# Stick-breaking attention with two heads per instruction, in PSUM tiles of two banks

## The chip, the cores and the metric

One core of a Trainium2 chip runs the whole program. Its engines are named as the profile names them: PE (TensorE, matmuls), PEld (the loading of its weights), DVE (VectorE), ACT (ScalarE), POOL (GpSimd) and SP (the engine whose queue issues most DMAs). Each engine works through its own queue in order. The metric is the time of one execution in microseconds (us).

## What is computed

Two transformer blocks over 512 tokens of width 1024, in f32: a mixer with two branches, a mixture of 16 experts, then a second block with retention, differential attention, cross attention and a feed-forward. The change touches one branch of the first mixer, stick-breaking attention with 8 heads of width 64 and blocks of 128 queries:

```python
def one_block(args):
    q_blk, blk = args
    z = jnp.einsum('bhqd,bhkd->bhqk', q_blk, k, preferred_element_type=jnp.float32) * scale
    q_pos = blk * QBLOCK + jnp.arange(QBLOCK)
    mask = key_pos[None, :] < q_pos[:, None]
    log_beta = jax.nn.log_sigmoid(z)
    log_keep = jnp.where(mask, jax.nn.log_sigmoid(-z), 0.0)
    later = jnp.concatenate([log_keep[..., 1:], jnp.zeros_like(log_keep[..., :1])], axis=-1)
    log_survive = lax.cumsum(later, axis=3, reverse=True)
    a = jnp.where(mask, jnp.exp(log_beta + log_survive), 0.0)
    return jnp.einsum('bhqk,bhkd->bhqd', a.astype(v.dtype), v)
```

The kernel uses that log_beta + log_survive = z minus the sum of softplus(z) over this key and all later ones.

## The kernel before

Products with weights are done in three float32r matmuls (high by high, high by low, low by high): `split` (lines 175 to 188) makes the two parts of a loaded weight, with a cast `whi` on ACT (L182) and a subtraction `wlo` on DVE (L183), each 128x1024; `mm3` (L200 to L202) issues the three matmuls; `hilo` (L265 to L267) splits an activation in the same way. `ws` (line 204) walks over tiles of 128 output columns, 24 matmuls of 512 columns each for the input projection. Below, a "filler" is one such matmul.

`sb_head` (lines 619 to 654) takes one head. Scores stand as keys by queries: for key block j (0 to 3) only the n = 512 - 128 j queries from that block on are computed, so a head has 512 + 384 + 256 + 128 = 1280 score columns. Per block: a score matmul (L628) in f32 over all 128 rows, where `sq_` holds one head's queries in 64 rows and zeros in the other 64; a bf16 matmul that adds the causal mask to the diagonal block (L629); a copy to `z` (L630, DVE); softplus as Abs, Exp, Ln on ACT (L632 to L634) and max-and-add on DVE (L635); the split into `ph` and `pl`. Then, per block, the running sum over later keys as matmuls with a triangle `tri` and ones `onesr` (L646, L647), the subtraction from z (L649, DVE), the exponential (L650, ACT), and the product with the values (L651, f32, 64 output rows).

`sb_head` runs for eight heads. Behind it in the program stand the gate projections (two `ws` of 8 tiles each, 384 fillers, evacuated by the ACT copies `gt`, L666), and then the two branch products (`w_branch_sb`, `w_branch_hg`). The instructions are not issued in program order: a scheduler of the framework puts each engine's queue in an order of its own, and so fillers of the gate projections stand between the matmuls of the heads. PSUM has 8 banks of 512 f32 columns: two each for the tags "mm" and "tp", and four that `four_banks` gives out again at each stage. The heads use those four singly (tag "at"). The second block's `diff_head` (line 1193) and `ret_pair` (line 1272) already take two heads at a time: score matmuls over 64 rows each (L1200, L1282), products with 64 output rows each (L1286), and one DVE instruction over both heads' banks (L1284).

Of the kernel before, what the change touches and what calls it, by code (L numbers as in the profile page):

```python
# [8 lines left out]
F32 = mybir.dt.float32  # L9
# [11 lines left out]
S = 512  # L21
# [7 lines left out]
NSL = 21  # L29
GX = (5, 6, 7, 8, 9)  # L30
# [53 lines left out]
def body(tc, a, out):  # L84
# [37 lines left out]
    def psum2():  # L122
        return banks[1][0].tile([128, 2, 512], F32, name="ps2", tag="at2", bufs=banks[1][2])
# [292 lines left out]
    slp = pool("slp", 1, stack=at)  # L416

    def slot(name):
        return slp.tile([128, S], F32, name=name, tag="sl", bufs=NSL)

# [165 lines left out]
    def ev_sq(t0):  # L586
        def f(t, o):
            for h in range(2):
                q = slot("sq")
                sq_[2 * (t0 + t) + h] = q  # L590
                G.memset(q[64 - 64 * h:128 - 64 * h, :], 0.0)
                A.activation(q[64 * h:64 * h + 64, :], o[64 * h:64 * h + 64, :], AF.Copy, scale=0.125)
        return f
# [18 lines left out]
    slp2 = pool("slp2", 1, stack=at)  # L612
    sbst = ExitStack()
    sb = pool("sb", 1, side="right", stack=sbst)
    COL = [0, 512, 896, 1152, 1280]

    last_exp = []

    def sb_head(h):
        t = h // 2  # L620
        z = sb.tile([128, 1280], F32, name="z", bufs=2)
        ph = sb.tile([128, 1280], F32R, name="ph", bufs=2)
        pl = sb.tile([128, 1280], F32R, name="pl", bufs=2)
        for j in range(4):
            n = S - 128 * j
            cc = slice(COL[j], COL[j + 1])
            o = psum("at")[:, :n]
            T.matmul(o, sk_[t][:, j * 128:(j + 1) * 128], sq_[h][:, j * 128:], start=True, stop=False)  # L628
            T.matmul(o[:, :128], identb, negsb, start=False, stop=True)  # L629
            V.tensor_copy(z[:, cc], o)  # L630
            e = sb.tile([128, S], F32, name="ea", bufs=3)[:, :n]
            A.activation(e, o, AF.Abs)  # L632
            A.activation(e, e, AF.Exp, scale=-1.0)
            A.activation(e, e, AF.Ln, bias=onec)  # L634
            V.scalar_tensor_tensor(e, z[:, cc], 0.0, e, op0=OP.max, op1=OP.add)  # L635
            hilo(ph[:, cc], pl[:, cc], e)
        y = psum("tp", name="ysbp")
        for j in range(4):
            n = S - 128 * j
            cc = slice(COL[j], COL[j + 1])  # L640
            o = psum("at")[:, :n]
            for i in range(j, 4):
                m = tri if i == j else onesr
                ci = slice(COL[i], COL[i + 1])
                oo = o[:, (i - j) * 128:]
                T.matmul(oo, m, ph[:, ci], start=(i == j), stop=False)  # L646
                T.matmul(oo, m, pl[:, ci], start=False, stop=(i == 3))  # L647
            w = sb.tile([128, S], F32, name="ea", bufs=3)[:, :n]
            V.tensor_sub(w, z[:, cc], o)  # L649
            last_exp[:] = [A.activation(w, w, AF.Exp)]  # L650
            T.matmul(y[64 * (h % 2):64 * (h % 2) + 64, 128 * j:], sv_[j][:, h * 64:(h + 1) * 64], w,  # L651
                     start=(j == 0), stop=(j == 3))
        p0 = 64 * (h % 2)
        hilo(ysb[0][p0:p0 + 64, t, :], ysb[1][p0:p0 + 64, t, :], y[p0:p0 + 64, :])

    for h in range(8):
        sb_head(h)
# [4 lines left out]
    def ev_gate(key):  # L662
        def f(t, o):
            n = t + (8 if key == "h" else 0)
            gt[key, t] = slot("gt") if n not in GX else slp2.tile([128, S], F32, name="gt2", bufs=len(GX))
            order(A.copy(gt[key, t], o), last_sk[0])  # L666
        return f
# [794 lines left out]
```

## Time and profile before

| | |
|---|---|
| runs | 1622.94, 1623.21, 1624.32 us, median 1623.21 |
| profiled execution | 1623.13 us |
| its span | 1621.3 us |
| busy in the span | PE 97%, PEld 75%, DVE 59%, ACT 51% |
| stick-breaking heads, 231.8 to 359.2 us | 127.4 us: PE 124.3, ACT 85.5, DVE 73.7 busy |
| the gate projections that are left, 359.2 to 391.4 us | 32.2 us: PE 32.2 busy |

A row of the profile gives an instruction's line, its engine, the tile written and the tiles read, and the shape. An f32 matmul shows as two records of one instruction, so its counts are double. A PE record lasts longer than its turn on the engine, since matmuls are pipelined: the turn is the distance from one start to the next. A bracket at the end of a timeline row gives the idle time of the engine before it and what ended it.

### The profile page before, as it was taken

How to read it: one execution, taken by the hardware profiler on the slowest of the kernel's cores; microseconds unless marked ns; L12 is line 12 of the kernel's file. 1: busy time of each engine (PE TensorE's matmuls, PEld its weight loads, DVE VectorE, ACT ScalarE, POOL GpSimd, SP SyncE). 2: the span in 40 equal slices, each digit the busy share in tenths (PEclk: the TensorE clock that was granted, in tenths of full speed). 3: DMA queues.
4: the chain of work that ended last, by engine and by line, in shares of the span. 5: the costliest groups of instructions: out<-in, count | busy, mean ns of one | idle time of the engine just before them, and what ended most of it. 6: DMA issues, size and time to landing. Idle time of an engine off the chain costs nothing. (4 is left out here: it accounts for less than half of the span.)

```text
span 1621.3 us, 20374 instructions
## 1 busy us (share of the span) xinstructions
PE 1579.7 (97%) x7631; PEld 1223.8 (75%) x7631; DVE 955.9 (59%) x1485; ACT 831.6 (51%) x1331; POOL 75.2 (5%) x92
## 2 busy tenths in 40 slices
PE   7999999999999999999989999999999999999999
PEld 6887776668878777776667667657878888888887
DVE  6459945643647899998855766456555433333221
ACT  5445556665335888888865664434444322323120
POOL 3000000000001211111110000000000000000000
PEclk9999999999999999999999999999999999999999
DMA  7230121123469999999974204224211333332331
GB/s 227 72 104 27 53 79 39 48 67 119 143 231 317 310 369 368 357 365 368 380 263 135 75 15 130 75 58 142 90 53 54 115 91 105 91 103 92 97 124 39
DMA packets 203070, 242.88 MB, mean 150 GB/s; under 512 B 10400, under 2 KB 133560, under 8 KB 202968
## 3 DMA queue, kind: packets, MB, share of 16 engines
q1 hardware_dynamic: 188800, 205.43, 38.1%
q0 software_dynamic: 7056, 24.27, 5.3%
q10 hardware_dynamic: 7112, 11.85, 2.5%
q8 instruction: 61, 1.00, 0.2%
q14 instruction: 41, 0.34, 0.1%
HBM read 223.69 MB, written 15.73 MB: 148 GB/s over the span
## 5 line engine op out<-in xcount | busy, mean ns | idle before, releaser
L183 DVE TENSOR_TENSOR wlo<-wraw,whi 128x1024 fp32r<-128x1024 f32 x210 | 256.0, 1223 | 284.9 <-ACT whi L182 275.5
L182 ACT CAST whi<-wraw 128x1024 fp32r<-128x1024 f32 x210 | 220.5, 1051 | 392.9 <-PE ps L201 276.2
L200 PE MATMUL ps<-hTh,whi 128*128 128x512 f32 (+1 forms) x912 | 349.8, 384 | 1.3 <-DVE fsg L1412 0.8
L201 PE MATMUL ps<-hTl,whi 128*128 128x512 f32 (+1 forms) x912 | 348.4, 382 | 0.8 <-DVE hTl L267 0.8
L202 PE MATMUL ps<-hTh,wlo 128*128 128x512 f32 (+1 forms) x912 | 347.7, 382 | 0.0
L183 DVE TENSOR_TENSOR wlo<-rx,whi 128x1024 fp32r<-128x1024 f32 x176 | 210.4, 1221 | 36.6 <-ACT whi L182 34.2
L182 ACT CAST whi<-rx 128x1024 fp32r<-128x1024 f32 x176 | 182.7, 1049 | 52.5 <-PE ps L202 31.3
L200 PEld LDWEIGHTS ps<-hTh,whi 128*128 128x128 f32 x912 | 172.2, 189 | 36.6 <-issue 3.3
L201 PEld LDWEIGHTS ps<-hTl,whi 128*128 128x128 f32 x912 | 172.2, 189 | 33.4 <-issue 2.2
L202 PEld LDWEIGHTS ps<-hTh,wlo 128*128 128x128 f32 x912 | 172.1, 189 | 31.3 <-issue 0.3
L200 PE MATMUL ps<-whi,XT 128*96 128x512 f32 x256 | 101.5, 396 | 1.8 <-ACTq L1045 1.8
L202 PE MATMUL ps<-whi,XT 128*96 128x512 f32 x256 | 102.0, 398 | 0.0
L201 PE MATMUL ps<-wlo,XT 128*96 128x512 f32 x256 | 100.9, 394 | 0.0
L200 PE MATMUL ps<-whi,hTh 128*128 128x512 f32 x192 | 77.4, 403 | 0.3 <-ACT hTh L266 0.2
L202 PE MATMUL ps<-whi,hTl 128*128 128x512 f32 x192 | 77.4, 403 | 0.0
L201 PE MATMUL ps<-wlo,hTh 128*128 128x512 f32 x192 | 76.6, 399 | 0.0
L200 PE MATMUL ps<-whi,aTh 128*128 128x512 f32 x176 | 68.5, 389 | 0.0
L202 PE MATMUL ps<-whi,aTl 128*128 128x512 f32 x176 | 68.5, 389 | 0.0
L201 PE MATMUL ps<-wlo,aTh 128*128 128x512 f32 x176 | 68.5, 389 | 0.0
L1412 DVE TENSOR_TENSOR fsg<-fsg,ps 128x512 f32<-128x512 f32 x22 | 15.1, 688 | 76.4 <-PE ps L202 76.4
L200 PEld LDWEIGHTS ps<-whi,XT 128*96 128x96 f32 x256 | 41.4, 162 | 18.4 <-ACTq L1045 2.2
L201 PEld LDWEIGHTS ps<-wlo,XT 128*96 128x96 f32 x256 | 41.5, 162 | 17.4 <-DVE wlo L183 0.3
(449 smaller groups left out, 2590.6 us busy)
## 6 DMA issues: line engine op xcount, KB each, us to landing
wraw<-in_w_in_dram SPq DMA_DIRECT2D x72, 512.0 KB
rx<-in_w_exp_gate_dram SPq DMA_DIRECT2D x58, 512.0 KB
rx<-in_w_exp_down_dram SPq DMA_DIRECT2D x58, 512.0 KB
rx<-in_w_exp_up_dram SPq DMA_DIRECT2D x52, 512.0 KB
wraw<-in_w_gate_dram SPq DMA_DIRECT2D x22, 512.0 KB
wraw<-in_w_up_dram SPq DMA_DIRECT2D x22, 512.0 KB
wraw<-in_w_down_dram SPq DMA_DIRECT2D x22, 512.0 KB
wraw<-in_w_out_dram SPq DMA_DIRECT2D x16, 512.0 KB
```

The source lines that it names most:

```text
L182: i1 = A.copy(hi, w)
L183: i2 = V.tensor_sub(lo, w, hi.bitcast(F32))
L200: T.matmul(o, lh, rh, start=first, stop=False)
L201: T.matmul(o, lh, rl, start=False, stop=False)
L202: T.matmul(o, ll, rh, start=False, stop=last)
L1412: V.tensor_mul(sg[t], sg[t], o)
```

## The change

Two heads now share an instruction. `sq_` keeps both heads of a pair as they come from the projection (one ACT instruction in place of two, no POOL memset), and the score matmuls of a pair read 64 rows each. Both write one PSUM tile of two banks (tag "sc"), and the running sums another (tag "run"); each tag has one buffer. The mask is added on DVE, in the instruction that moves the scores to `z`; Abs reads `z` in place of PSUM. Softplus, split, subtraction and exponential work on [128, 2, n], up to 1024 columns. The key blocks run from 3 to 0, each with its running sum and exponential, and the products with the values come after all four. `z`, `ph` and `pl` have two buffers for blocks 2 and 3 and one for blocks 0 and 1. The exponential is written over `z`. The gates take their slots from one pool.

```diff
-    def psum2():
-        return banks[1][0].tile([128, 2, 512], F32, name="ps2", tag="at2", bufs=banks[1][2])
+    def psum2(tag="at2"):
+        return banks[1][0].tile([128, 2, 512], F32, name=tag, tag=tag, bufs=banks[1][2])
...
+    mask = yp.tile([128, S], F32, name="mask")
+    G.memset(mask[:, 128:], 0.0)
+    V.tensor_copy(mask[:, :128], negsb)
...
-            for h in range(2):
-                q = slot("sq")
-                sq_[2 * (t0 + t) + h] = q
-                G.memset(q[64 - 64 * h:128 - 64 * h, :], 0.0)
-                A.activation(q[64 * h:64 * h + 64, :], o[64 * h:64 * h + 64, :], AF.Copy, scale=0.125)
+            sq_[t0 + t] = slot("sq")
+            A.activation(sq_[t0 + t], o, AF.Copy, scale=0.125)
...
+    four_banks("at1", 1)
...
+    def sb_pair(t):
+        y = psum("tp", name="ysbp")
+        z, ph, pl = {}, {}, {}
+        for j in (3, 2, 1, 0):
+            c0, n = 128 * j, S - 128 * j
+            o = psum2("sc")[:, :, :n]
+            for h in range(2):
+                T.matmul(o[:, h], sk_[t][hs[h], c0:c0 + 128], sq_[t][hs[h], c0:], start=True, stop=True)
+            z[j] = sb.tile([128, 2, n], F32, name=f"z{j}", bufs=2 if j > 1 else 1)
+            V.tensor_add(z[j], o, mask[:, None, :n].to_broadcast([128, 2, n]))
+            ph[j], pl[j] = (sb.tile([128, 2, n], F32R, name=f"p{q}{j}", bufs=2 if j > 1 else 1) for q in "hl")
+            e = sb.tile([128, 2, S], F32, name="ea", bufs=2)[:, :, :n]
+            A.activation(e, z[j], AF.Abs)
+            A.activation(e, e, AF.Exp, scale=-1.0)
+            A.activation(e, e, AF.Ln, bias=onec)
+            V.scalar_tensor_tensor(e, z[j], 0.0, e, op0=OP.max, op1=OP.add)
+            hilo(ph[j], pl[j], e)
+            o = psum2("run")[:, :, :n]
+            for h in range(2):
+                for i in range(j, 4):
+                    m = tri if i == j else onesr
+                    oo = o[:, h, (i - j) * 128:]
+                    T.matmul(oo, m, ph[i][:, h], start=(i == j), stop=False)
+                    T.matmul(oo, m, pl[i][:, h], start=False, stop=(i == 3))
+            V.tensor_sub(z[j], z[j], o)
+            last_exp[:] = [A.activation(z[j], z[j], AF.Exp)]
+        for j in range(4):
+            for h in range(2):
+                T.matmul(y[hs[h], 128 * j:], sv_[j][:, (2 * t + h) * 64:(2 * t + h + 1) * 64], z[j][:, h],
+                         start=(j == 0), stop=(j == 3))
+        hilo(ysb[0][:, t, :], ysb[1][:, t, :], y)
...
+    four_banks("at2")
```

In the queues below, a number behind a tile's name only tells one buffer's use from another's.

PE's queue where one head ends and the next begins, before: the scores of the next head, the masks, and the products with the values of the last one (ysbp).

```order
L628 MATMUL ps<-sq,sk 128x512
L651 MATMUL ysbp<-ea,sv 64x512
L629 LDWEIGHTS identb
L629 MATMUL ps<-negsb,identb 128x128
L628 MATMUL ps<-sq,sk 128x384
L651 MATMUL ysbp<-ea,sv 64x384
L651 MATMUL ysbp<-ea,sv 64x256
```

The same queue where the third pair ends, with the change (L646 is the product with the values, L640 and L641 are the running sums).

```order
L646 MATMUL ysbp<-z_2258,sv 64x512 x2
L646 MATMUL ysbp<-z_2229,sv 64x384 x2
L646 MATMUL ysbp<-z_2204,sv 64x256 x2
L646 MATMUL ysbp<-z_2183,sv 64x128 x2
L640 MATMUL run<-ph_2325,tri 128x256
L641 MATMUL run<-pl_2326,tri 128x256
```

The products of a pair now stand together, two heads side by side, ahead of the next pair's running sum of block 2. Counted over the whole queue, 239 of the 384 gate fillers stand between the first and the last matmul of the heads before, and 135 with the change; 145 and 249 stand behind.

ACT's queue at a head's end, before: the last casts, a weight split, a gate copy, the four exponentials and the cast of the head's output.

```order
L266 CAST ph<-ea 128x256
L182 CAST whi<-wraw 128x1024
L266 CAST ph<-ea 128x128
L666 COPY gt<-ps 128x512
L650 ACTIVATE ea<-ea 128x512
L650 ACTIVATE ea<-ea 128x384
L650 ACTIVATE ea<-ea 128x256
L650 ACTIVATE ea<-ea 128x128
L266 CAST ysb_270<-ysbp 64x512
```

The same queue where the second pair ends and the third is on its way, with the change (z_2139 is block 0 of the second pair; z_2183 and z_2204 are blocks 3 and 2 of the third).

```order
L265 CAST ph_2185<-ea 128x256
L181 CAST whi<-wraw 128x1024
L630 ACTIVATE ea<-z_2204 128x2x256
L661 COPY gt<-ps 128x512
L631 ACTIVATE ea<-ea 128x2x256
L632 ACTIVATE ea<-ea,onec 128x2x256
L265 CAST ph_2206<-ea 128x512
L643 ACTIVATE z_2139<-z_2139 128x1024
L643 ACTIVATE z_2183<-z_2183 128x256
L265 CAST ysb_270<-ysbp 128x512
```

The exponential of a pair's block 0 stands behind the next pair's softplus of block 2.

DVE's queue at the same place, with the change (L633 max-and-add, L642 subtraction of the running sum, L627 mask and move).

```order
L266 TENSOR_TENSOR pl_2142<-ea,ph_2141 128x1024
L266 TENSOR_TENSOR pl_2186<-ea,ph_2185 128x256
L182 TENSOR_TENSOR wlo<-wraw,whi 128x1024
L633 SCALAR_TENSOR_TENSOR ea<-z_2204,ea 128x2x256
L642 TENSOR_TENSOR z_2139<-z_2139,run 128x1024
L266 TENSOR_TENSOR pl_2207<-ea,ph_2206 128x512
L642 TENSOR_TENSOR z_2183<-z_2183,run 128x256
L627 TENSOR_TENSOR z_2229<-sc,mask 128x768
```

The subtraction for block 0 of the second pair (z_2139) stands behind the max-and-add of block 2 of the third (z_2204).

## Rows read from the trace of the kernel before

**Rows 1.** Page: the span, and each engine's busy time, share and instructions.

```profile
span 1621.3 us, 20374 instructions
PE 1579.7 (97%) x7631; PEld 1223.8 (75%) x7631; DVE 955.9 (59%) x1485; ACT 831.6 (51%) x1331; POOL 75.2 (5%) x92
```

**Rows 2.** Busy time by stretch: the heads, then the remaining gate tiles.

```profile
core 0: us, PE busy (x) PEld busy (x) DVE busy (x) ACT busy (x) POOL busy (x), PEclk, DMA share, GB/s
231.80:359.20 127.40, 124.33 (x563) 84.56 (x562) 73.65 (x145) 85.47 (x190) 0.00 (x0) 1.00 0.15 43
359.20:391.40 32.20, 32.20 (x143) 26.65 (x142) 8.05 (x7) 16.76 (x27) 0.00 (x0) 1.00 0.51 163
```

**Rows 3.** PE timeline (start us, us), second head: scores, products with values.

```profile
245.13 1.10 PE L628 MATMUL ps<-sq,sk 128*128 128x512 f32 x2 [0.26 <-DVE ea L649]
246.15 2.37 PE L651 MATMUL ysbp<-ea,sv 128*64 128x512 f32 x8
248.45 0.23 PE L629 MATMUL ps<-negsb,identb 128*128 128x128 bf16 x1
248.52 0.86 PE L628 MATMUL ps<-sq,sk 128*128 128x384 f32 x2
...
250.13 0.47 PE L202 MATMUL ps<-hTh,wlo 128*128 128x512 f32 x1
```

**Rows 4.** PE timeline, retention: scores and products of two heads together.

```profile
1024.48 1.77 PE L1282 MATMUL ps<-rq,rk 64*128 64x512 f32 x8
...
1027.86 1.73 PE L1286 MATMUL ps<-pp,rv 128*64 128x512 f32 x8 [0.94 <-DVE pp L1284]
1029.52 0.92 PE L1282 MATMUL ps<-rq,rk 64*128 64x256 f32 x8
...
1031.03 0.87 PE L1286 MATMUL ps<-pp,rv 128*64 128x256 f32 x8
```

**Rows 5.** PE timeline, second head: running sums of 512 and 384 columns.

```profile
254.35 0.39 PE L647 MATMUL ps<-pl,tri 128*128 128x512 f32 x1
254.59 0.34 PE L646 MATMUL ps<-ph,onesr 128*128 128x384 f32 x1
254.76 0.34 PE L646 MATMUL ps<-ph,tri 128*128 128x384 f32 x1
```

**Rows 6.** Instructions of a line: ns min/median/max, first and last start, forms.

```profile
L633 ACT ACTIVATE ea<-ea x32: 300/474/633, 235.9 to 349.2; 128x512 f32<-128x512 f32 x8, 128x384 f32<-128x384 f32 x8, 128x256 f32<-128x256 f32 x8, 128x128 f32<-128x128 f32 x8
L634 ACT ACTIVATE ea<-ea,onec x32: 398/566/723, 236.8 to 350.4; 128x512 f32<-128x512 f32 x8, 128x384 f32<-128x384 f32 x8, 128x256 f32<-128x256 f32 x8, 128x128 f32<-128x128 f32 x8
L1284 DVE TENSOR_TENSOR pp<-ps,dec x16: 411/818/1225, 1026.6 to 1083.9; 128x1024 f32<-128x1024 f32 x4, 128x768 f32<-128x768 f32 x4, 128x512 f32<-128x512 f32 x4, 128x256 f32<-128x256 f32 x4
```

**Rows 7.** Page, groups: busy us, mean ns, idle before: the weight splits.

```profile
L183 DVE TENSOR_TENSOR wlo<-wraw,whi 128x1024 fp32r<-128x1024 f32 x210 | 256.0, 1223 | 284.9 <-ACT whi L182 275.5
L182 ACT CAST whi<-wraw 128x1024 fp32r<-128x1024 f32 x210 | 220.5, 1051 | 392.9 <-PE ps L201 276.2
```

**Rows 8.** PE timeline: two long waits of PE, in the experts and in retention.

```profile
811.86 0.55 PE L992 MATMUL ps<-ident,act 96*128 96x96 f32 x4 [2.31 <-DVE act L985]
...
813.68 0.63 PE L200 MATMUL ps<-whi,ah 128*96 128x512 f32 x1
814.11 0.63 PE L201 MATMUL ps<-wlo,ah 128*96 128x512 f32 x1
...
1067.11 1.77 PE L1282 MATMUL ps<-rq,rk 64*128 64x512 f32 x8 [1.25 <-DVE rk L1269]
```

**Rows 9.** Busy time by stretch (columns as Rows 2): around those waits, and the experts.

```profile
700.00:750.00 50.00, 50.00 (x241) 35.49 (x240) 46.26 (x47) 42.10 (x52) 6.28 (x5) 1.00 1.05 364
...
810.00:815.00 5.00, 2.57 (x10) 1.71 (x11) 3.50 (x5) 1.42 (x2) 0.00 (x0) 0.83 1.05 333
...
1060.00:1090.00 30.00, 28.27 (x128) 15.64 (x126) 15.28 (x22) 8.27 (x13) 0.00 (x0) 1.00 0.17 49
```

**Rows 10.** Timeline of SP's queue: the first load of an expert's weights.

```profile
450.55 0.37 SPq L1029 DMA_DIRECT2D rx<-in_w_exp_gate_dram  x1
```

More of the change, by code (lines that the diff above doesn't have):

```diff
@@ L28 @@
 OVER = 10
-NSL = 21
-GX = (5, 6, 7, 8, 9)
+NSL = 20
 NRX = 8
@@ L610, in body @@
     hgst.close()
-    slp2 = pool("slp2", 1, stack=at)
     sbst = ExitStack()
     sb = pool("sb", 1, side="right", stack=sbst)
-    COL = [0, 512, 896, 1152, 1280]
+    four_banks("at1", 1)
+    hs = [slice(64 * h, 64 * h + 64) for h in range(2)]
     last_exp = []
[L619 to L632, printed above, removed]
+    def sb_pair(t):
[11 more added lines that the diff above has]
+            A.activation(e, z[j], AF.Abs)
@@ L633, in sb_head @@
             A.activation(e, e, AF.Exp, scale=-1.0)
             A.activation(e, e, AF.Ln, bias=onec)
-            V.scalar_tensor_tensor(e, z[:, cc], 0.0, e, op0=OP.max, op1=OP.add)
-            hilo(ph[:, cc], pl[:, cc], e)
-        y = psum("tp", name="ysbp")
-        for j in range(4):
[L639 to L657, printed above, removed]
+            V.scalar_tensor_tensor(e, z[j], 0.0, e, op0=OP.max, op1=OP.add)
[7 more added lines that the diff above has]
+                    T.matmul(oo, m, pl[i][:, h], start=False, stop=(i == 3))
@@ L660, in body @@
+            V.tensor_sub(z[j], z[j], o)
+            last_exp[:] = [A.activation(z[j], z[j], AF.Exp)]
+        for j in range(4):
+            for h in range(2):
+                T.matmul(y[hs[h], 128 * j:], sv_[j][:, (2 * t + h) * 64:(2 * t + h + 1) * 64], z[j][:, h],
+                         start=(j == 0), stop=(j == 3))
+        hilo(ysb[0][:, t, :], ysb[1][:, t, :], y)
+    for t in range(4):
+        sb_pair(t)
+    four_banks("at2")
     gt = {}
@@ L663, in f @@
         def f(t, o):
-            n = t + (8 if key == "h" else 0)
-            gt[key, t] = slot("gt") if n not in GX else slp2.tile([128, S], F32, name="gt2", bufs=len(GX))
+            gt[key, t] = slot("gt")
             order(A.copy(gt[key, t], o), last_sk[0])
```

## The prediction, on record before the result

> **What bounds the kernel now.** I read the page first: PE is busy 97% of a span of 1621.3 us [rows 1]. The reader is to see that only work taken from PE, or PE's waits, can move the end. Then the stretches: the heads take 127.4 us with PE busy 124.3, ACT 85.5 and DVE 73.7, and the remaining gate tiles 32.2 us with PE busy throughout, 143 matmuls at 0.225 us each [rows 2]. So PE bounds both stretches, but a busy PE isn't a PE at its peak, so I counted its turns. The stretch ends with the last gate tile: what counts is heads plus remaining fillers, 159.6 us.
>
> **PE's work.** A head's scores before: 1.02 us for block 0 (245.13 to 246.15) and 1.61 for the other three with their masks (248.52 to 250.13), together 2.63; its products with the values run from 246.15 to 248.45, 2.30 [rows 3]. The changed kernel uses the forms of retention, and there two heads' scores of 512 and 384 columns took 1.77 us and those of 256 and 128 columns 0.92, together 2.69; the products 1.73 and 0.87, together 2.60 [rows 4]. Two heads apart would take 5.26 and 4.60. So heads over 64 rows each, and over 64 output rows each, run side by side, and a pair saves 2.57 + 2.00 = 4.57 us; four pairs 18.3 us. The masks go with it. The running sums keep their number and size: turns of 0.24 us for 512 columns and 0.17 for 384 [rows 5], so the 16 of a pair's block 0 take at most 4 x (0.24 + 3 x 0.17) = 3.0 us; all 40 of a pair (4 of 512 columns, 8 of 384, 12 of 256, 16 of 128), with 0.12 and 0.13 estimated for the short ones, about 5.9.
>
> **ACT and DVE.** Twice the columns per instruction save only the fixed part. Exp takes 300 ns for 128 columns and 633 for 512, so 0.867 ns a column: by that line 411, 633, 855 and 1077 for 256 to 1024, 2.98 us a pair; Abs and the last exponential I take as the same, and Ln by its own row (398 to 723) at 3.33. The cast I price as Exp too; at 1024 columns 1051 ns is shown for a cast [rows 6, 7]. ACT: 4 x 2.98 + 3.33 = 15.2 us a pair. DVE has four operations of two operands; the paired form took 411 to 1225 ns, 3.27 us a pair each, 13.1 in all [rows 6]. That the mask is added in place of a plain copy costs nothing in this price. The order adds, per pair, an output cast and a gate copy on ACT (0.6 each, estimated from the 633 row), one weight split (1.05 ACT, 1.22 DVE) [rows 7] and 28 fillers on PE. Sums per pair: PE 2.7 + 2.6 + 5.9 + 28 x 0.225 = 17.5; ACT 17.5; DVE about 15. PE loses its lead: three engines stand nearly level, and the waits between them decide.
>
> **The loop of one pair.** Blocks 0 and 1 have one buffer, sc and run one each, so I walked the order from one pair's last exponential (of block 0, end at 0) to the next one's, with the durations above. Products of blocks 0 and 1 until 1.9 free z1; mask and move of block 1 on DVE until 2.9; output cast, after all products, until 3.4; then ACT runs Abs and Exp of block 1 (5.1), the exponential of block 2 (5.8), Ln (6.7), Abs of block 0 (7.8), the cast of block 1 (8.6), Exp and Ln of block 0 (10.8), the next pair's block 3 (12.1), the cast of block 0 (DVE's max-and-add came at 12.1; 13.2), the exponential of block 1 (14.1), the next cast (14.5), a weight cast (15.5), Abs of the next block 2, a gate copy, Exp, Ln (18.1). DVE's max-and-add of that block ends at 18.8, and only behind it stands block 0's subtraction (20.0); the exponential ends at 21.1. The running sum of block 0, ready by 17.6, doesn't set this; the place of the subtraction behind the next pair's block 2 does. PE waits some 3.5 us in such a round, in pieces of at most 1.5. Take **21 us a pair**.
>
> The first pair has no predecessor; by the same walk its block 0 ends 22 us after the first score matmul. The last has no successor's work in its way: 20 us, and 2.7 for its products. Heads: 22 + 2 x 21 + 20 + 2.7 = 87 us. ACT would be busy about 80% of that, before 67% [rows 2].
>
> **The sum.** Heads 127.4 to 87: -40.4. But only 135 fillers run inside in place of 239, and 104 more stand behind: + 104 x 0.225 = 23.4. Sum **-17 us**. It agrees with what PE loses in work (18.3) less a little more waiting. Against the profiled execution, 1623.1 (span 1621.3), this is 1606; the median of the runs is 1623.2, so the same.
>
> Edits that I cost at nothing: one ACT instruction of 128 rows in place of two of 64 for sq, and the POOL memsets, lie in stretches where PE or DVE is the late one; the mask is made once at the start. Cover gone, they would be worth 2 us at most. The gate tiles behind the heads need an ACT cast (1.05) and a DVE subtraction (1.22) per 24 fillers of 5.4 us [rows 7], so the longer tail stays on PE. The tables of rows give no price for a handoff between engines beyond what lies in the durations; between 0 and 0.1 us for each of some 20 in a round, I take 0 and keep 4 x 2 = 8 us for the range.
>
> **Rivals.**
>
> *The queues overlap better than my walk.* If ACT's own sum bounds a pair (17.5), the heads take 4 x 17.5 + 4 = 74 us, and the time is 1593. For it: nothing is on ACT that could not be earlier. Against: a queue is worked in order, and the order is read. 0.07.
>
> *PE's clock falls.* In the experts PE waited 2.31 us, and the stretch 810 to 815 us was granted 0.83: matmuls then took turns of 0.43 us, so the 1.2 GHz level; in retention PE waited 1.25 us and the grant stayed at 1.00 [rows 8, 9]. My waits (up to 1.5) lie between. If each round had such a spell of some 4 us, it would cost 2 us, 8 in all: 1614. 0.13, with the case that the handoffs cost as much. The Trainium skill, TensorE: Matmul & The Clock Gate, section "A second HAM failure mode: psum-queue depth-cycling", describes a kernel whose PE idles briefly between matmul groups as it goes round its PSUM buffers, and whose clock swings for it. Before, the whole stretch of the heads shows 1.00 [rows 2], so that rule has not acted on the four single banks; it would take back up to 8 us here.
>
> *The gain is lost in the experts.* There DMA is at 1.05 of its share [rows 9], so if DMA alone set that stage, an earlier start would not help. Against: the first expert load is issued at 450.55 us [rows 10], behind the branch products that end later than the gates, so the stage moves as a whole, and PE is busy 50 of 50 us in it too. Price: all 17, time 1623. 0.07.
>
> *Slower: the loop through the single buffers doesn't overlap.* In a row, a pair's steps are: block 0 about 14 us, block 1 10.5, block 2 7.7, block 3 4.9 and the products 2.6, 40 us. My round of 21 has nearly half of it hidden. The forecast turns at 87 + 17 = 104 us for the heads, a round of 25 to 26 us. If half the overlap fails (30.5 a round), the heads take 125 and the time is 1644. For it: one buffer each for sc, run, z0, z1; evacuation on DVE alone. Against: the scheduler put fillers where PE would wait, and the waits in the walk are few. 0.06. The Trainium skill, TensorEngine Tiling (Array Packing), section Performance Considerations, under "PSUM Bottleneck", warns of this side: tiles side by side speed up TensorE and not the emptying of PSUM, and both ScalarE and VectorE should empty it. The change goes against it, since Abs no longer reads PSUM; by my rows DVE still has 6 of 21 us free, so I hold it to this rival.
>
> *It doesn't do what it says:* two heads don't run side by side in this stage. Then PE needs 4.57 us more in a round, of which 3.5 fall into its waits: some 5 us over four pairs, 1611. 0.04, since the forms are those of retention.
>
> **How the numbers follow.** My own forecast has 0.63, at 1606, with a range of its own of 1599 to 1611. A measurement of this kernel tells 0.2%, 3.2 us, from no change. Faster: 0.63 + 0.07 + 0.13 + 0.04 = 0.87; the same: 0.07; slower: 0.06. The range 1597 to 1618 leaves out the better overlap, the lost gain and the serial loop, 0.20.
>
> **What would show it.** Right: in the changed profile the pairs' scores and products take about 2.7 and 2.6 us a pair; the heads last 80 to 95 us with ACT busy about four fifths; 249 matmuls follow at 0.225; everything behind starts some 17 us earlier, the first expert load at about 433. Wrong: PE waits for DVE at sc or run more than 6 us a round (the serial loop), a grant under 1.00 in the heads (the clock), an expert stage longer than before (lost gain), or a subtraction of block 0 that doesn't end last in its round (my walk).

## The result and the profile after

The changed kernel takes 1605.23 us (median of 4 runs, 1603.15 to 1606.79), the kernel before 1623.45 beside it: a ratio of 0.9886 with a 95% interval of 0.9874 to 0.9898, so 18.2 us less. The forecast was 1606.0. The profiled execution took 1603.82 us.

The page of the changed kernel, its first rows, as [rows 1] of before:

```profile
span 1602.0 us, 20081 instructions
PE 1561.0 (97%) x7599; PEld 1213.7 (76%) x7599; DVE 946.3 (59%) x1418; ACT 818.8 (51%) x1243; POOL 70.9 (4%) x85
PEclk9999999999999999999999999999999999999999
```

PE is as busy as before as a share; it has less to do. (In the changed kernel the lines of the heads' stage have other numbers: L625 scores, L627 mask and move, L630 to L632 Abs, Exp, Ln, L633 max-and-add, L640 and L641 running sums, L642 subtraction, L643 last exponential, L646 products; L199 to L201 are the three matmuls of a gate tile.)

The stretches of the changed kernel by pair (columns: from and to in us, length, then busy us and instructions of PE, PEld, DVE, ACT and POOL, granted clock, DMA share, GB/s), and behind them the remaining gate tiles, as [rows 2] of before:

```profile
232.80:254.80 22.00, 20.59 (x107) 13.73 (x106) 17.38 (x24) 20.11 (x32) 0.00 (x0) 1.00 0.15 45
254.80:274.50 19.70, 18.78 (x100) 12.71 (x100) 14.99 (x20) 16.47 (x24) 0.00 (x0) 1.00 0.11 32
274.50:295.17 20.67, 19.81 (x105) 13.60 (x106) 14.30 (x19) 16.03 (x23) 0.00 (x0) 1.00 0.09 27
295.17:317.30 22.13, 21.45 (x115) 15.05 (x115) 12.45 (x13) 15.81 (x21) 0.00 (x0) 1.00 0.16 48
317.30:373.80 56.50, 56.50 (x251) 46.78 (x250) 12.94 (x11) 23.45 (x35) 0.00 (x0) 1.00 0.42 130
```

The reader is to see that a round takes 19.7 to 20.7 us, the heads 84.5 in place of 127.1 (the 127.4 of [rows 2] begin 0.26 us before the first score matmul), ACT is busy 68.4 of these (81%), the clock is granted in full, and PE's idle time is under 1 us in a round (19.70 less 18.78). (Here and below, a round goes from one pair's first product with the values to the next pair's.) What counts for the end is the whole stage, from the first score matmul to the first branch product that reads the heads' output: 232.06 to 391.67 before, 159.6 us, and 232.79 to 373.81 after, **141.0 us**. The two stages whole, before and after:

```profile
232.06:391.67 159.61, 156.54 (x705) 111.22 (x704) 81.70 (x152) 102.23 (x217) 0.00 (x0) 1.00 0.22 67
```
```profile
232.79:373.81 141.02, 137.15 (x673) 101.89 (x673) 72.07 (x84) 91.89 (x133) 0.00 (x0) 1.00 0.25 75
```

The stage is 18.6 us shorter: PE's busy time in it fell by 19.4 and its idle time grew from 3.1 to 3.9. It started 0.7 later, and the stages behind it made up for that, as told below.

### The profile page after: what moved, and what is told of

It is laid out like the page before. It is cut to its first block, busy times and chain, and to the rows that moved or that the text cites. A ratio compares the mean times of both kernels' runs of the same rounds, so it can differ in the third digit from the quotient of the medians.

```text
span 1602.0 us, 20081 instructions
## 1 busy us (share of the span) xinstructions
PE 1561.0 (97%) x7599; PEld 1213.7 (76%) x7599; DVE 946.3 (59%) x1418; ACT 818.8 (51%) x1243; POOL 70.9 (4%) x85
## 5 line engine op out<-in xcount | busy, mean ns | idle before, releaser
L199 PE MATMUL ps<-hTh,whi 128*128 128x512 f32 (+1 forms) x912 | 349.0, 383 | 1.3 <-DVE fsg L1407 0.8
L201 PE MATMUL ps<-hTh,wlo 128*128 128x512 f32 (+1 forms) x912 | 347.5, 381 | 0.0
L199 PEld LDWEIGHTS ps<-hTh,whi 128*128 128x128 f32 x912 | 172.1, 189 | 38.8 <-issue 4.7
L201 PEld LDWEIGHTS ps<-hTh,wlo 128*128 128x128 f32 x912 | 172.0, 189 | 32.7 <-issue 1.5
L199 PE MATMUL ps<-whi,XT 128*96 128x512 f32 x256 | 101.5, 397 | 1.8 <-ACTq L1040 1.8
L201 PE MATMUL ps<-whi,XT 128*96 128x512 f32 x256 | 102.0, 398 | 0.0
L199 PE MATMUL ps<-whi,hTh 128*128 128x512 f32 x192 | 77.5, 403 | 0.1
L201 PE MATMUL ps<-whi,hTl 128*128 128x512 f32 x192 | 77.1, 401 | 0.0
L199 PE MATMUL ps<-whi,aTh 128*128 128x512 f32 x176 | 68.5, 389 | 0.0
L201 PE MATMUL ps<-whi,aTl 128*128 128x512 f32 x176 | 68.5, 389 | 0.0
L199 PEld LDWEIGHTS ps<-whi,XT 128*96 128x96 f32 x256 | 41.3, 161 | 18.5 <-ACTq L1040 2.2
L200 PEld LDWEIGHTS ps<-wlo,XT 128*96 128x96 f32 x256 | 41.4, 162 | 17.3
```

The costliest lines, as they stand in the source:

```text
L199: T.matmul(o, lh, rh, start=first, stop=False)
L200: T.matmul(o, lh, rl, start=False, stop=False)
L201: T.matmul(o, ll, rh, start=False, stop=last)
```

## Is it PE's work, or the loop and its instructions?

Two theories stand against each other. **P:** PE's work governs. The stage lasts as long as PE has matmuls for, plus a little idle time, and the 18 us are those of scores and products that now run side by side, and of the masks that PE no longer adds. **W:** the loop through ACT and DVE governs, as my walk had it, and PE has some 3.5 us idle in each round to take in other work. A variant, **F**, gives the gain to the fewer and wider instructions of ACT and DVE. Of each kernel below I give the median time, its ratio to the kernel before run on the same chip (1623.7 to 1624.9 there), and the length of the stage, which single profiles show better than the whole time does.

### Heads apart on PE

```
-    V.tensor_copy(mask[:, :128], negsb)
+    V.memset(mask[:, :128], 0.0)
...
-                T.matmul(o[:, h], sk_[t][hs[h], c0:c0 + 128], sq_[t][hs[h], c0:], start=True, stop=True)
+                T.matmul(o[:, h], sk_[t][hs[h], c0:c0 + 128], sq_[t][hs[h], c0:], start=True, stop=False)
+                T.matmul(o[:, h, :128], identb, negsb, start=False, stop=True)
...
-        for j in range(4):
-            for h in range(2):
+        for h in range(2):
+            for j in range(4):
                 T.matmul(y[hs[h], 128 * j:], ...
```

> The changed kernel with its two heads no longer side by side on PE: between the two heads' score matmuls stands each head's 128-column mask matmul (as in the kernel before; DVE then adds a mask of zeros), and the products run one head after the other. ACT and DVE do what they do in the changed kernel. Theory P (PE's work governs): scores and products of a pair back to 5.26 + 4.60 us, +4.57 a pair and 18.3 in all; head stage with the gate tiles behind it from 142 to 160 us, end at 1623. Theory W (the loop through ACT and DVE governs, PE has idle time in each round): most of it falls into PE's waits, 2.0 a pair of products lies on the loop; stage 147, end at 1610 to 1613.

Measured: 1622.49 us, ratio 0.9993 (0.9983 to 1.0002). Judged by the time, the whole gain is gone, with ACT and DVE as wide as in the changed kernel. The stage took 156.7 us (233.37 to 390.07): it is 2.9 shorter than before, and started 1.3 later. By pair, and the gate tiles behind:

```profile
233.40:262.50 29.10, 28.77 (x133) 18.99 (x132) 18.15 (x25) 21.28 (x32) 0.00 (x0) 1.00 0.13 37
262.50:285.60 23.10, 23.10 (x107) 15.07 (x107) 13.30 (x18) 16.84 (x24) 0.00 (x0) 1.00 0.08 23
285.60:308.30 22.70, 22.37 (x105) 14.35 (x104) 14.96 (x20) 15.57 (x24) 0.00 (x0) 1.00 0.08 24
308.30:333.60 25.30, 25.12 (x115) 16.68 (x115) 12.22 (x13) 16.41 (x21) 0.00 (x0) 1.00 0.15 42
333.60:390.00 56.40, 56.40 (x249) 46.71 (x250) 12.95 (x11) 23.08 (x33) 0.00 (x0) 1.00 0.42 131
```

PE's busy time in the stage sums to 155.8 us, against 137.1 in the changed kernel: 18.6 more, where the prediction had 18.3. Idle time fell from 3.9 to 0.8 us, so all that the waits took in was 3.0. P holds: the second pair has no idle PE time at all here.

How the two heads share PE is seen in the groups of matmuls by shape (columns: line, engine, operation, names, shapes, count, then busy us, mean ns of one). The changed kernel:

```profile
L625 PE MATMUL sc<-sq,sk 64*128 64x512 f32 x16 | 4.5, 641 | 0.0
L646 PE MATMUL ysbp<-z,sv 128*64 128x512 f32 x16 | 4.3, 618 | 0.8 <-ACT z L643 0.7
```

and the one with the heads apart:

```profile
L625 PE MATMUL sc<-sq,sk 64*128 64x512 f32 x16 | 9.0, 641 | 0.0
L647 PE MATMUL ysbp<-z,sv 128*64 128x512 f32 x16 | 8.6, 618 | 0.7 <-ACT z L644 0.7
```

The mean of one matmul is the same, 641 and 618 ns; the time that the group keeps PE busy is half. Side by side is read from the busy time, not from the mean.

### Only the products apart

```
-        for j in range(4):
-            for h in range(2):
+        for h in range(2):
+            for j in range(4):
```

> The changed kernel with only the products one head after the other (a turn of 3.93 us in place of 2.37, by the run with all apart, 1.56 a pair). Theory P: 4 x 1.6 = +6 us in the stage, less up to 1 for idle time, end 1610 to 1611. Theory W (idle time takes it in): within 2 us of the changed kernel.

Measured: 1612.12 us, ratio 0.9922 (0.9901 to 0.9943); stage 147.0, 5.9 longer than in the changed kernel. P again, 1 us above its range in the time: of the 17.3 us between the changed kernel and the one with all apart, 6.9 are the products'; the rest, 10.4, by subtraction, is the scores' with their masks (predicted 4 x 2.57 = 10.3). By the stages the two shares are 5.9 and 9.7. The intervals of the times are 3 to 7 us wide for one such run, so that a match within 0.1 us is chance. How much of the scores' share is the masks alone is seen further down, where they come back as matmuls and the heads stay side by side: about 3 us, in a run that also changes who reads the scores.

### One head per ACT and DVE instruction

```
-            V.tensor_add(z[j], o, mask[:, None, :n].to_broadcast([128, 2, n]))
+            for h in range(2):
+                V.tensor_add(z[j][:, h], o[:, h], mask[:, :n])
...
-            A.activation(e, z[j], AF.Abs)
...
+            for h in range(2):
+                A.activation(e[:, h], z[j][:, h], AF.Abs)
...
-            V.tensor_sub(z[j], z[j], o)
+            for h in range(2):
+                V.tensor_sub(z[j][:, h], z[j][:, h], o[:, h])
...
```

Exp, Ln, max-and-add, the high and low parts and the last exponential go in the same way.

> The changed kernel with every ACT and DVE instruction of the heads on one head's columns (two of half the width in place of one); PE's matmuls as they are. ACT gets 20 more instructions a pair at 0.189 us fixed each (the Exp line of the kernel before), +3.8 us; DVE 16 more at 0.14, +2.2. Theory F (the gain came from fewer, wider instructions): the end goes back to 1618 or more. Theory P (PE's work governs): rounds grow by up to 4 us, but gate matmuls fill them and fewer stand behind, so the end stays within 1603 to 1609, stage 142 to 146 us. The shorter pieces may also overlap better, which would give below 1605.

Measured: 1613.15 us, ratio 0.9941 (0.9925 to 0.9958), stage 146.9. By the time alone this lies between the theories: 8 us lost. But the rounds became *shorter*, 18.5, 18.3 and 18.7 us, and the heads 82.2, though ACT has 20 instructions more in each. What grew is PE's busy time, 142.4 us in the stage against 137.1. Two of its groups show where:

```profile
L625 PE MATMUL sc<-sq,sk 64*128 64x384 f32 x16 | 6.4, 535 | 0.0
L649 PE MATMUL ysbp<-z,sv 128*64 128x512 f32 x16 | 6.0, 618 | 0.0
```

These were 3.7 and 4.3 us in the changed kernel. Since each head now frees its half of the score tile, and gets its exponentials, at its own time, the order puts other matmuls between the two heads' scores of 384 columns, and the products of the last pair wait for one head after the other (4.28 us for the 16, from 310.49 to 314.77, in place of 2.38): a part of the side-by-side work has come apart. That is a reading of one trace, so the next run tests it.

### One head per instruction only between mask and running sum

```
-            A.activation(e, z[j], AF.Abs)
...
-            hilo(ph[j], pl[j], e)
+            for h in range(2):
+                A.activation(e[:, h], z[j][:, h], AF.Abs)
...
+                hilo(ph[j][:, h], pl[j][:, h], e[:, h])
```

> The changed kernel with one head's columns per instruction only between mask and running sum (Abs, Exp, Ln, max-and-add, high and low part: 16 more ACT instructions a pair, 3.0 us, and 8 more on DVE, 1.1 us); mask, subtraction and last exponential stay two heads wide, so that both heads' scores and products are released together and stay side by side on PE, but for five pairs of scores that stand apart in this kernel's order (0.35 to 0.56 us each, 1.7 in sum). Theory P (what the narrow forms cost, 1613 in place of 1605, was PE's work: 142.4 us busy in the stage in place of 137.1): end 1605 to 1608. Theory F (the instructions' fixed parts on ACT and DVE cost it themselves): 16 of 20 of it, 1611 or more.

Measured: 1607.12 us, ratio 0.9894 (0.9875 to 0.9912), stage 143.0. It has 16 of the 20 extra ACT instructions of a pair, and of the 5.8 us that the stage lost with all of them it loses 2.0. PE's busy time is 140.6, so 3.5 more than in the changed kernel (the parted scores, which were expected at 1.7), and its idle time is 1.5 less. F falls. The width of ACT's and DVE's instructions matters here because a two-head instruction releases both heads at once, and with it they stand together on PE; the fixed part of the instructions was paid in time that costs nothing.

### Both undone

The two edits above together: the scores and products apart, and one head per instruction throughout.

```
+                T.matmul(o[:, h, :128], identb, negsb, start=False, stop=True)
...
+                V.tensor_add(z[j][:, h], o[:, h], mask[:, :n])
```

> Both undone, the loop over pairs with its double and single buffers kept. Theory P: as with the matmuls apart alone, 1623, stage 160. Theory F: 1618 or more with the narrow forms alone, and no more here. If the two add up, 1605 + both single differences; if they stand in for each other (idle PE time that the one makes takes in the work of the other), less than that.

Measured: 1622.37 us, ratio 0.9989 (0.9980 to 0.9999), stage 157.1. The narrow forms cost 8 us where the heads are side by side and nothing where they are apart anyway. That is what P, with the reading above, requires.

## Does the round matter at all?

### Shorter rounds

```
-            e = sb.tile([128, 2, S], F32, name="ea", bufs=2)[:, :, :n]
+            e = sb.tile([128, 2, S if j < 3 else n], F32, name="ea" if j < 3 else "eb", bufs=2 if j < 3 else 1)[:, :, :n]
...
             for h in range(2):
                 for i in range(j, 4):
-                    T.matmul(oo, m, ph[i][:, h], start=(i == j), stop=False)
-                    T.matmul(oo, m, pl[i][:, h], start=False, stop=(i == 3))
+                    T.matmul(..., ph[i][:, h], start=(i == j), stop=False)
+            for h in range(2):
+                for i in range(j, 4):
+                    T.matmul(..., pl[i][:, h], start=False, stop=(i == 3))
```

The reason for this run is the end of a round in the changed kernel, here the third pair's block 0, from the order in time of PE, ACT and DVE (columns: start us, length us, engine, line, operation, names, shapes, count, idle time before it and what ended it):

```profile
292.41 0.27 PE L641 MATMUL run<-pl,onesr 128*128 128x128 f32 x1
```
```profile
290.12 0.63 ACT L630 ACTIVATE ea<-z 128x512 f32<-128x512 f32 x1 [0.98 <-DVE pl L266]
294.06 1.06 ACT L643 ACTIVATE z<-z 128x1024 f32<-128x1024 f32 x1 [0.51 <-DVE z L642]
```
```profile
292.20 0.69 DVE L633 SCALAR_TENSOR_TENSOR ea<-z,ea 128x512 f32<-128x512 f32 x1 [1.78 <-ACT ea L632]
292.81 1.21 DVE L642 TENSOR_TENSOR z<-z,run 128x1024 f32<-128x1024 f32 x1
```

The subtraction of block 0 (L642) does stand behind the next pair's max-and-add (L633), as the walk said. But that max-and-add is late because ACT idled 0.98 us before it could reuse one of the two `ea` buffers, and the running sum ended at 292.68, only 0.13 us before the subtraction began: three things end together.

> The changed kernel with a buffer of its own for block 3's exponentials, so that the next pair's block 2 doesn't wait for block 0's cast (ACT idles 0.98 us there in the changed kernel's round), and with the running sums' high parts all ahead of the low parts, so that PE does 8 of block 0's 16 matmuls while DVE makes the low part. Theory as predicted (block 0's subtraction is late because it stands behind the next pair's max-and-add): no shorter round, 20 to 20.7 us, end 1604 to 1606. Theory R (the running sum and the ring of two buffers set it too: in the changed kernel the last running-sum matmul ends 0.13 us before that subtraction starts): rounds shorter by 1 to 1.4 us, and as a part of it is filled already, end 1600 to 1603.

Measured: 1604.78 us, ratio 0.9887 (0.9871 to 0.9904), stage 139.9. The rounds went to 18.9, 19.5 and 19.1 us, so theory R is right about the round. Yet the time stayed: the heads are 2.5 us shorter, 6 matmuls fewer stand inside them, and the whole stage is 1.1 shorter, by PE's idle time (2.6 in place of 3.9). Which of the two edits shortened the round was not separated.

### Longer rounds

```
-            z[j] = sb.tile([128, 2, n], F32, name=f"z{j}", bufs=2 if j > 1 else 1)
+            z[j] = sb.tile([128, 2, n], F32, name=f"z{j}", bufs=1)
...
-            ph[j], pl[j] = (sb.tile([128, 2, n], F32R, name=f"p{q}{j}", bufs=2 if j > 1 else 1) for q in "hl")
+            ph[j], pl[j] = (sb.tile([128, 2, n], F32R, name=f"p{q}{j}", bufs=1) for q in "hl")
```

> The changed kernel with one buffer for every block's z, high and low part (before: two for blocks 2 and 3). Rival of the serial loop: the next pair's blocks 3 and 2 can't begin until this pair's products and running sums are done, their 12.6 us come to the round: over 26 us, heads above 104, end 1623 or more. If only a part is exposed and gate matmuls fill the rest: rounds 22 to 25, end 1606 to 1612.

Measured: 1604.60 us, ratio 0.9877 (0.9858 to 0.9896), stage 140.9. Both expectations were wrong about the time. The rounds are 24.4 to 25.5 us and the heads 99.3, 15 longer than in the changed kernel, and it costs nothing. The stretches (columns as above):

```profile
256.30:280.70 24.40, 23.81 (x121) 16.12 (x120) 15.42 (x19) 17.42 (x26) 0.00 (x0) 1.00 0.15 44
333.00:374.50 41.50, 41.50 (x183) 34.38 (x184) 9.27 (x8) 18.96 (x29) 0.00 (x0) 1.00 0.45 146
```

PE is busy 23.81 of 24.40 us in a round: 201 gate matmuls stand inside the heads in place of 135, and 183 behind in place of 249. The scheduler puts a gate matmul wherever the loop leaves a hole, so the length of the round is no price as long as gate tiles are left.

### No gate matmuls inside

```
+    hold = []
...
     def mm3(o, lh, ll, rh, rl, first, last):
-        T.matmul(o, lh, rh, start=first, stop=False)
+        m = T.matmul(o, lh, rh, start=first, stop=False)
+        if hold:
+            order(m, hold[0])
...
+    hold[:] = last_exp
     ws(w_in, 8, 3584, 8, hT, S, ev_gate("s"))
     ws(w_in, 8, 4608, 8, hT, S, ev_gate("h"))
+    hold[:] = []
```

> The changed kernel with every matmul of the gate tiles held back until the last exponential of the heads: the loop alone, 384 gate matmuls behind it (86.4 us at 0.225). Walk as predicted (ACT and DVE set the round, gate matmuls only fill): rounds still 18.5 to 20 us, heads 80 to 85, end 1605 + 135 x 0.225 less a little = 1628 to 1635. If gate matmuls ahead of the running sums lengthen the round: 16 to 18 us, heads 70 to 75, end 1620 to 1627. The clock: PE idles some 8 to 10 us in each round, in pieces of 1 to 4 us; if such waits lower the grant, as the wait of 2.31 us in the experts did, the heads show less than 1.00 and matmuls at 0.43 us; if not, 1.00.

Measured: 1639.72 us, ratio 1.0093 (1.0068 to 1.0117), longer than either expectation; the rounds are 21.4 to 23.0 us, and but for five matmuls just ahead of the last products no gate tile stands in them. What the trace shows for it is the clock. The heads, the gate tiles behind, and the first 8 us in pieces of 2:

```profile
232.83:324.64 91.81, 71.41 (x295) 46.96 (x294) 53.44 (x68) 60.21 (x85) 0.00 (x0) 0.72 0.02 7
324.64:410.60 85.96, 85.96 (x379) 71.19 (x380) 19.07 (x16) 34.31 (x48) 0.00 (x0) 1.00 0.37 116
```
```profile
232.00:234.00 2.00, 1.47 (x10) 0.85 (x11) 0.63 (x2) 1.28 (x2) 0.00 (x0) 1.00 0.40 119
234.00:236.00 2.00, 0.88 (x6) 0.45 (x8) 2.00 (x3) 1.83 (x5) 0.00 (x0) 1.00 0.00 0
236.00:238.00 2.00, 2.00 (x10) 1.04 (x6) 1.30 (x3) 1.89 (x5) 0.00 (x0) 0.57 0.87 252
238.00:240.00 2.00, 2.00 (x5) 0.50 (x5) 1.29 (x3) 2.00 (x4) 0.00 (x0) 0.50 0.05 14
```
```profile
233.85 0.70 PE L629 MATMUL sc<-sq,sk 64*128 64x256 f32 x4 [0.53 <-DVE z L631]
235.67 1.08 PE L629 MATMUL sc<-sq,sk 64*128 64x384 f32 x4 [1.12 <-DVE z L631]
237.96 2.08 PE L629 MATMUL sc<-sq,sk 64*128 64x512 f32 x4
```

Two waits of 0.53 and 1.12 us with little between them, and the grant goes to 0.50, the 1.2 GHz level: the scores of 512 columns, 1.13 us for the four at full clock, take 2.08. The mean grant over the heads is 0.72. So the stage is 36.8 us longer than in the changed kernel: 29.5 are gate matmuls that now stand behind (85.96 in place of 56.50), and the heads are 7.3 longer in spite of having less to do. That the clock alone made them longer is not shown, since no run has the loop without gate matmuls at 1.00. The gate matmuls do two things in the heads: they fill, and they keep the clock at 1.00. The rule of the Trainium skill, TensorE: Matmul & The Clock Gate, section "A second HAM failure mode: psum-queue depth-cycling", on a clock that swings when PE idles briefly between groups of matmuls, is what this kernel shows; the changed kernel, whose loop goes round the same banks with gate matmuls in the holes, does not.

## Other ways through PSUM, and less work for PE

### Scores read in PSUM by ACT and DVE

```
+            for h in range(2):
+                T.matmul(o[:, h, :128], identb, negsb, start=False, stop=True)
-            V.tensor_add(z[j], o, mask[:, None, :n].to_broadcast([128, 2, n]))
+            V.tensor_copy(z[j], o)
...
-            A.activation(e, z[j], AF.Abs)
+            A.activation(e, o, AF.Abs)
```

> The changed kernel with the masks as matmuls again, so that both ACT (Abs) and DVE (a plain copy) read the scores in PSUM and work side by side on a block. Theory P: 8 more matmuls of 128 columns a pair cost PE 0.6 to 1.2 us, 2.5 to 5 in all, and a loop that gets shorter gives nothing: end 1606 to 1610. The rule on the emptying of PSUM by both engines, were it what limits here: shorter rounds, and an end below 1603.

Measured: 1610.12 us, ratio 0.9915 (0.9898 to 0.9931), 3.0 above the changed kernel beside it; stage 144.1. The records of the 32 mask matmuls take 4.6 us, partly beside others; PE's busy time in the stage grew by 1.5 and its idle time by 1.6 (138.6 and 5.5 us). Nothing came back for it; the rounds are 20.1 to 21.9 us. P, at the upper end of its range, though half of the loss is waiting.

### Fewer matmuls in the running sums

```
...
-            ph[j], pl[j] = (sb.tile([128, 2, n], F32R, name=f"p{q}{j}", bufs=2 if j > 1 else 1) for q in "hl")
+            ph[j], pl[j] = (sb.tile([128, 2, n], F32R, name=f"p{q}{j}", bufs=1) for q in "hl")
...
             for h in range(2):
-                for i in range(j, 4):
...
+                T.matmul(o[:, h], tri, ph[j][:, h], start=True, stop=False)
+                T.matmul(o[:, h], tri, pl[j][:, h], start=False, stop=(j == 3))
+                if j < 3:
+                    T.matmul(o[:, h, 128:], onesr[0:33, :], car[j + 1][0:33, h], start=False, stop=True)
             V.tensor_sub(z[j], z[j], o)
+            if j:
+                A.copy(car[j][0:1], o[0:1])
+                V.tensor_sub(car[j][32:33], o[0:1], car[j][0:1].bitcast(F32))
```

> The changed kernel with less PE work in the running sums: the sum over all later blocks is the first row of the next block's running sum, so that row is taken over (high part into row 0, low part into row 32 of a tile of zeros) and spread by one matmul of 33 rows, in place of two matmuls for every later block: 28 in place of 40 matmuls a pair, by 0.24, 0.17, 0.12 and 0.07 us for 512 to 128 columns 0.88 us a head less, 7.0 in all. ACT and DVE get three casts and three subtractions of one row more a pair (1.9 and 2.0 us), and the high and low parts have one buffer each. Theory P (PE's work governs, the rounds' length doesn't): rounds may grow to 22 us and more, more gate matmuls stand inside, the stage 134 to 137 in place of 141, end 1598 to 1601. Theory W (the loop through ACT and DVE governs): no gain or a loss, 1605 or more.

Measured: 1602.38 us (4 runs, 1600.36 to 1605.12), ratio 0.9870 (0.9854 to 0.9886); the changed kernel on the same chip took 1607.08. The stage is 136.4 us. Columns as above, the pairs of this kernel:

```profile
232.50:256.80 24.30, 23.35 (x102) 14.23 (x101) 19.12 (x26) 21.57 (x35) 0.00 (x0) 1.00 0.15 42
256.80:277.70 20.90, 20.71 (x93) 12.78 (x92) 17.07 (x22) 18.66 (x29) 0.00 (x0) 1.00 0.10 29
277.70:298.75 21.05, 20.61 (x95) 13.04 (x96) 17.14 (x23) 18.75 (x29) 0.00 (x0) 1.00 0.17 50
298.75:323.30 24.55, 24.44 (x112) 15.88 (x113) 16.28 (x18) 18.47 (x26) 0.00 (x0) 1.00 0.22 65
```

Every round is longer than in the changed kernel, ACT has more to do, and the stage is 4.6 us shorter. W would have it longer, so this is P: what PE does in the stage counts, the loop's length doesn't. The gain is 4.6 and not the 7.0 of the count. Of it 2.4 are PE's busy time (134.7 in place of 137.1) and 2.2 its idle time (1.7 in place of 3.9), since more gate matmuls stand in the holes; a likely reason why the work fell by 2.4 only stands in the last section. This version is the fastest of all by its median.

### The changed kernel again

> The changed kernel beside the two above: 1603 to 1607, the stage 141 us.

No edit. Measured: 1607.08 us, ratio 0.9892 (0.9875 to 0.9908), stage 141.0. This profile and the first one of the same kernel have spans of 1605.7 and 1602.0 us. The heads start 1.1 later in it, the experts' first matmuls of L987 are level again (524.3 and 524.4), the last stand 2.2 apart (794.6 and 792.4) and retention's first scores 4.1 (1008.5 and 1004.4): the two differ in the expert stage and behind it. PE's waits for the experts' activations there, in the changed kernel and in its repetition (columns: engine, what it waited for, us in total, times, longest):

```profile
PE ps L987 <- DVE act L980: 2.3, 1, 2.3
```
```profile
PE ps L987 <- DVE act L980: 4.0, 3, 2.3
```

The kernel before had 4.0 too. So of the 19.3 us between the two profiled executions, the stage gives 18.6 less 0.7 for its later start, and of the rest some part is this wait (1.7), which comes and goes between runs of one kernel.

### All stages side by side

The length of the stage and PE's part of it, in us, one profile each:

| kernel | stage | PE busy | PE idle |
|---|---|---|---|
| before | 159.6 | 156.5 | 3.1 |
| changed | 141.0 | 137.1 | 3.9 |
| heads apart | 156.7 | 155.9 | 0.8 |
| heads apart, one head per instruction | 157.1 | 157.1 | 0.0 |
| products apart | 147.0 | 143.3 | 3.6 |
| one head per instruction | 146.9 | 142.4 | 4.4 |
| the same between mask and running sum | 143.0 | 140.6 | 2.4 |
| shorter rounds | 139.9 | 137.3 | 2.6 |
| longer rounds | 140.9 | 138.4 | 2.4 |
| scores read by ACT and DVE | 144.1 | 138.6 | 5.5 |
| fewer matmuls in the running sums | 136.4 | 134.7 | 1.7 |
| no gate matmuls inside (clock 0.72 in the heads) | 177.8 | 157.4 | 20.4 |

As long as the clock is at 1.00, PE's busy time runs from 134.7 to 157.1 us and the stage goes with it, whatever the rounds do; the idle time stays between 0.0 and 5.5.

## Why the prediction was right, point by point

**PE's work: right.** The saving of 4.57 us a pair, 18.3 in all, was measured as 19.4 in PE's busy time against the kernel before, 18.6 against the one with the heads apart, and 17.3 in the time. Products were a little cheaper than taken from retention [rows 4]: 2.38 us for the 16 of a pair, not 2.60. The running sums were dearer, 6.7 to 6.8 us busy in a round in place of 5.9, and the scores 3.2 in place of 2.7; the sums are the same matmuls in both kernels, so the saving stands. That the forms of retention run side by side here too is shown by the halved busy time.

**The durations of ACT and DVE: right.** The line through 128 and 512 columns [rows 6] gave 411, 633, 855 and 1077 ns; ACT's Exp took 398, 737 (the median) and 1060, and DVE's subtraction 411 to 1221.

**The loop: right in length, by a mechanism that doesn't set the time.** 22.0 for the first pair (predicted 22), 19.7 and 20.7 (21), 84.5 for the heads (87), ACT busy 81%. The place of the subtraction is as the walk had it, but it is not the only thing that sets it: the walk had the running sum ready 1.2 us before (17.6 against 18.8), where it ended 0.13 before, and with that sum and the `ea` buffers eased the rounds went from 20.0 to 19.2 in the mean. And the step that failed is "PE waits some 3.5 us in such a round": it waits 0.9. In the round of 19.7 us stand 28 gate matmuls, as priced; the round is 1.3 shorter than the walk's 21, and the pair's own matmuls keep PE busy 18.78 - 28 x 0.225 = 12.5 us, where the prediction summed 2.7 + 2.6 + 5.9 = 11.2. In the round of 20.7 us stand 33, five more than priced, and the pair's own matmuls take 12.4.

**The sum: right, for a reason it gave only second.** Heads less 40.4, gate matmuls behind plus 23.4 gave -17; measured were 127.1 - 84.5 = 42.6 less in the heads and 24.0 more behind them (359.20 to 391.67 before, 317.30 to 373.81 after), so -18.6. The heads' length and the matmuls behind them are not two independent terms, though: when the rounds were made 15 us longer in all, or 2.5 shorter, the second gave back what the first took. The one sentence that the sum "agrees with what PE loses in work" was the cause (by the rows, 19.4 less work and 0.8 more waiting); the walk only told how much of the filling lies inside.

**Edits at nothing: within the 2 us that were named.** The heads start at 232.79 in place of 232.06, and at 233.85 in the repetition; 0.7 to 1.8 us ahead of them is the price, or chance of the order, and no run separates it. The first expert load was forecast at 433 and issued at 432.65, so the stage did move as a whole: the first branch product came 17.9 us sooner, and the gain was not lost behind it.

**The rivals.** *Doesn't run side by side* was priced at 1611, because 3.5 of 4.57 us were to vanish in PE's waits. Built, it took 1622.5: the failed step on PE's waits again, and the rival was worth the whole gain. *The serial loop* was priced at 1644 with a turn at rounds of 25 to 26 us; with rounds of 24.4 to 25.5 and 15 us more in the heads the time was 1604.6. The price took 135 gate matmuls inside as fixed, where 201 went in. *The clock* was the rival nearest to being real: taken without gate matmuls, waits of 0.53 and 1.12 us lowered the grant, shorter than the 1.25 that left it at 1.00 in retention [rows 8, 9]. In the changed kernel the gate matmuls stand in those holes, and the grant is 1.00. *Better overlap* was priced at 1593 by heads of 74 us; shorter rounds (18.9 to 19.5) gave nothing, so a better overlap could not have brought it: what was there to gain is PE's idle time, 3.9 us in the stage. The rule cited from the Trainium skill, TensorEngine Tiling (Array Packing), section Performance Considerations, that both engines should empty PSUM, did not bind: with both reading the scores, and the mask matmuls that this takes, the kernel was 3.0 us slower beside it and its rounds were no shorter.

## What to carry to other kernels

Where a scheduler fills an engine's holes with independent work, count that engine's work over the whole stage, loop and filler together, and take the idle time from rows; the loop's length is a price only when the filler runs out, or when the clock falls for want of it. Two heads stay side by side on PE most surely where what releases them, and what they release, is one instruction for both; with two instructions other matmuls came between some of them here. The next gain here was again in PE's own work: a row carried over in place of matmuls that sum it anew.

## What the runs showed of the hardware

- After two PE waits of 0.53 and 1.12 us, one behind the other, the grant went from 1.00 to 0.50, and in the loop without filler it swung (0.50 from 240 to 250 us, 0.99 from 260 to 270, 0.69 from 270 to 280) with a mean of 0.72, where a single wait of 1.25 us had left it at 1.00 in retention [rows 8, 9].
- A matmul over 64 rows, or into 64 output columns, has the same mean whether the other half of the array works or not (641 and 618 ns); only the busy time of the group tells (4.5 and 9.0 us for 16).
- A matmul of 33 rows was dearer here than one of 128. The carried rows, and the sums over full blocks that they replace in the changed kernel:

```profile
L644 PE MATMUL run<-car,onesr 33*128 33x384 f32 x8 | 3.5, 440 | 0.0
```
```profile
L640 PE MATMUL run<-ph,onesr 128*128 128x384 f32 x8 | 2.7, 339 | 0.0
```

Records last longer than turns, so here are turns too, of the carried rows (from 268.14 to 268.45 us) and of a sum over a full block of 256 columns in the changed kernel (from 269.24 to 269.36):

```profile
267.88 0.33 PE L642 MATMUL run<-pl,tri 128*128 128x384 f32 x1
268.14 0.38 PE L644 MATMUL run<-car,onesr 33*128 33x256 f32 x1
268.45 0.44 PE L641 MATMUL run<-ph,tri 128*128 128x384 f32 x1
```
```profile
269.24 0.28 PE L640 MATMUL run<-ph,onesr 128*128 128x256 f32 x1
269.36 0.28 PE L641 MATMUL run<-pl,onesr 128*128 128x256 f32 x1
```

That is 0.31 us in place of 0.12, and the matmul ahead of it took 0.26 where 384 columns otherwise took 0.17 [rows 5]. The count of 7.0 priced the carried rows like full ones; with 24 of them, this is where most of the 4.6 us between 7.0 and 2.4 went, as an estimate: 24 x (0.19 + 0.09) = 6.7 at most, less where a score matmul starts beside one. No run separates it.
